# Inverting the 16-column diagonal blocks of a delta-rule stage with one block per partition, laid out through DRAM, and moving large elementwise products off GpSimd

## The chip, the cores and the metric

One core of a Trainium2 chip runs the whole kernel. The metric is device time in microseconds (us) of one execution. Engines are named as in the profile: PE is TensorE, PEld its weight loads, DVE is VectorE, ACT is ScalarE, POOL is GpSimd, SP is SyncE, whose instruction queue (SPq) issues nearly all DMAs of this kernel.

## The reference

A two-layer decoder trunk on 1024 tokens of width 1024: an MLA attention layer, an RWKV-7 layer, a feed-forward net behind each, and in both layers attention over 256 memory tokens. The change lies in the RWKV-7 layer, whose heart is a recurrence over tokens for 12 heads of width 64:

```
def step(S, inp):
    r_t, w_t, k_t, v_t, a_t, b_t = inp
    sa = jnp.einsum("bhij,bhj->bhi", S, a_t)
    S = S * w_t[:, :, None, :] + sa[..., None] * b_t[:, :, None, :] + v_t[..., None] * k_t[:, :, None, :]
    y = jnp.einsum("bhij,bhj->bhi", S, r_t)
    return S, y
```

Its result `y` is normalised per head, scaled and shifted (`rwkv_gn_g`, `rwkv_gn_b`), given a term `(r*k*r_k).sum()*v`, and gated.

## The kernel before

The recurrence is computed in chunks of `CH` = 64 tokens. A unit `n` (12 in all, `N = 2 * NPAIR`) covers two pairs of heads (`u`), four chunks (`c`, `NC` = 4) and, on the two halves of the partitions (`A`, `B`, in code `R, hd in HD`), two heads of a pair: 16 matrices of 64x64. Inside a chunk the recurrence becomes a triangular system, so every unit needs the inverse of 16 unit-triangular 64x64 matrices (identity minus the tile `N`).

The stage has these functions, in the order that the loop at its end (L1197 to L1221) calls them for each unit: `sequence(n)` carries the state through the four chunks, on PE with DVE copies between; `invert(n + 1)` makes `X`, the inverse that `sequence(n + 1)` multiplies by at L1152; `prepare(n + 2)` loads and normalises; `finish(n)` does the group norm and writes to `o_d`; `products(n + 2)` calls `unit`, which makes the scaled operands (`F`, `AR`, `BKz`) and, by the matmuls `ps_ga` (L1038), the tile `N`. Between them stand pieces of independent work, handed out by `fill` and the table `FILL`: input projections (`ps_in`), memory attention (`ps_ms`), parts of the output projection (`ps_o`), nearly all of it matmuls over 512 columns at L149 to L151.

The program is ordered by a scheduler, which places every instruction on its engine by planned durations. An engine then runs its instructions strictly in that order: one that waits holds all that stand behind it. The same holds for SPq: a DMA that waits for its source or buffer holds the DMAs behind it.

`invert` before has two parts. First it inverts the 16x16 diagonal blocks of all matrices (L1064 to L1090): POOL masks `N` to its diagonal blocks (`nx`), DVE sums them together (`ndg`), and then 15 elimination steps run in four groups. For each group ACT scales rows with columns of an identity (`Z`, L1077), a matmul with the constant `B16` spreads them over the 16 partitions of a block (`ps_z`, L1079), ACT copies the result out (`Nr`, L1081), and POOL does a product (`xtmp`, L1086) and a sum (`Xs`, L1087) for each step, 128 partitions by 120 down to 8 elements. DVE spreads the result to `X` (L1089). Then two rounds (masks `M1`, `M2`) join blocks of 16 into 32 and 64, each with a DVE transpose `XT` (L1095), matmuls `ps_q` (L1099) and `ps_x` (L1105), and DVE products.

Other products on POOL in the stage: `pm` in `shifted` (L702), the softmax weights of memory attention (L773), `F` and half of `AR` in `unit` (L1026 to L1028), and two on `o` in `finish` (L1193, L1194).

Of the kernel before, what the change touches and what calls it, by code (L numbers as in the profile page):

```python
# [10 lines left out]
F32 = mybir.dt.float32  # L11
# [9 lines left out]
P = 128  # L21
# [45 lines left out]
class Trunk:  # L67
# [588 lines left out]
    def rwkv(self, rows_src):  # L656
        nc, a, sm = self.nc, self.a, self.sm
        res_src = rows_src
        NC = QT // CH
# [5 lines left out]
        with ExitStack() as so:  # L665
# [24 lines left out]
            def shifted(ps, m, h, out, pr=None):  # L690

                pm = shp.tile([P, H], F32, name="pm", bufs=1)
                if pr is None:
                    pr = shp.tile([P, H + 1], F32, name="pr", bufs=2)
                    nc.scalar.copy(pr[:, 1:], ps)
                if h == 0:
                    nc.gpsimd.memset(pr[:, 0:1], 0.0)  # L697
                    carry[m] = sm.tile([P, 1], F32, name="carry", tag="carry", bufs=8)
                    nc.gpsimd.tensor_copy(carry[m], pr[:, H : H + 1])
                else:  # L700
                    nc.gpsimd.tensor_copy(pr[:, 0:1], carry[m])
                nc.gpsimd.tensor_scalar(pm, pr[:, 0:H], self.col("mu", m), None, op0=ALU.mult)  # L702
                nc.vector.scalar_tensor_tensor(out, pr[:, 1:], omu[:, m : m + 1], pm, op0=ALU.mult, op1=ALU.add)

            def weights(m, pool=None):
# [40 lines left out]
            def remember():  # L746
# [10 lines left out]
                def soft(n):  # L757
                    u, i = n // 4, n % 4
                    m, q, pe = u // 2, qs[u % 2], part(pes, n)
                    if i == 0:  # L760
                        nc.sync.dma_start(q, q_d[:, m, (u % 2) * H : (u % 2 + 1) * H])
                    ps = psm.tile([P, 2, NM], F32, name="ps_ms", tag="mm")
                    for hd in range(2):
                        nc.tensor.matmul(ps[:, hd, :], q[:, i * P : (i + 1) * P], mk[:, 2 * m + hd, :], start=True, stop=True)
                    nc.scalar.copy(pe, ps)
                    mx = sm.tile([P, 2], F32, name="mmx")
                    l = sm.tile([P, 2], F32, name="ml")
                    nc.vector.tensor_reduce(mx, pe, axis=AX.X, op=ALU.max)
                    nc.vector.tensor_scalar(mx, mx, -MEM_SCALE, None, op0=ALU.mult)
                    for hd in range(2):  # L770
                        nc.scalar.activation(pe[:, hd, :], pe[:, hd, :], AF.Exp, bias=mx[:, hd : hd + 1], scale=MEM_SCALE, accum_out=l[:, hd : hd + 1])
                    nc.vector.reciprocal(l, l)
                    nc.gpsimd.tensor_mul(pe, pe, l[:, :, None].broadcast_to([P, 2, NM]))  # L773

                def weigh(n):
                    u, i = n // 4, n % 4
# [129 lines left out]
            with ExitStack() as s:  # L906
# [12 lines left out]
                MM, blk, B16 = (cm[:, i, :] for i in (0, 2, 3))  # L919
# [4 lines left out]
                m16 = kp.tile([P, 80], F32, name="m16")  # L924
                nc.sync.dma_start(m16, a["consts"][:, 2690:2770])
                eye16, dg16 = m16[:, 0:16], m16[:, 16:80]
# [5 lines left out]
                self.pad(kp, 32)  # L932
                self.pad(tp, 96)
                ARK = [kp.tile([P, 2, NC, 2, P], F32, name=f"ARK{i}") for i in range(2)]
                BKz = kp.tile([P, NC, 2, P], F32, name="BKz")
                for t in [cmp_, BKz]:
                    nc.gpsimd.memset(t, 0.0)
                c3 = lambda t: t.rearrange("p (c t) -> p c t", t=CH)
                t1 = lambda name, bufs=1, tag=None: tp.tile([P, QT], F32, name=name, tag=tag or name, bufs=bufs)
                DU = {}  # L940
# [65 lines left out]
                def unit(d, u, rkv, sga, kk):  # L1006
# [16 lines left out]
                    AR = tp.tile([P, NC, 2, CH], F32, name="AR")  # L1023
                    F = tp.tile([P, NC, 2, CH], F32, name="F")
                    nc.vector.scalar_tensor_tensor(AR[:, :, 0, :], c3(kk), -1.0, pt[:, :, 0:CH], op0=ALU.mult, op1=ALU.mult)
                    nc.gpsimd.tensor_mul(F[:, :, 0, :], c3(kk), c3(at))  # L1026
                    nc.gpsimd.tensor_mul(F[:, :, 1, :], c3(k), c3(tk))
                    nc.gpsimd.tensor_mul(AR[:, :, 1, :], c3(r), pt[:, :, 1:])  # L1028

                    bz = lambda hd: bkz[:, :, hd, :].rearrange("p c (h t) -> p c h t", h=2)  # L1030
                    nc.vector.tensor_mul(bz(0)[A], F[A], c3(pi)[A][:, :, None, :].broadcast_to([64, NC, 2, CH]))
# [23 lines left out]
                    nc.vector.tensor_mul(d["bv"][:, u, :], pbv, v)  # L1055


                def invert(n):
                    d = DU[n]
                    U8 = 2 * NC  # L1060
                    N = d["N"]
                    n8 = N.rearrange("p u c t -> p (u c) t")

                    nx = up.tile([P, U8, 4, 16], F32, name="nx", bufs=1)  # L1064
                    nc.gpsimd.tensor_mul(nx.rearrange("p a b t -> p a (b t)"), n8, dg16[:, None, :].broadcast_to([P, U8, 64]))
                    ndg = up.tile([P, U8, 16], F32, name="ndg", bufs=1)
                    nc.vector.tensor_reduce(ndg, nx.rearrange("p a b t -> p a t b"), axis=AX.X, op=ALU.add)
                    Xs = up.tile([P, U8, 16], F32, name="Xs", bufs=1)
                    nc.gpsimd.tensor_copy(Xs, eye16[:, None, :].broadcast_to([P, U8, 16]))
                    for t0 in range(0, 15, 4):  # L1070

                        tn, w0 = min(4, 15 - t0), 15 - t0
                        n0 = tn * U8 * w0
                        rows = lambda t: t[:, :n0].rearrange("p (j a t) -> p j a t", j=tn, a=U8)
                        Z = up.tile([P, 480], F32, name="Z", bufs=1)
                        for j in range(tn):
                            nc.scalar.activation(rows(Z)[:, j], ndg[:, :, t0 + 1 :], AF.Copy, scale=eye16[:, t0 + j : t0 + j + 1])  # L1077
                        pz = psi.tile([P, 480], F32, name="ps_z", tag="i")
                        nc.tensor.matmul(pz[:, :n0], B16, Z[:, :n0], start=True, stop=True)  # L1079
                        Nr = up.tile([P, 480], F32, name="Nr")  # L1080
                        nc.scalar.copy(Nr[:, :n0], pz[:, :n0])  # L1081
                        for j in range(tn):
                            t = t0 + j
                            w = 15 - t
                            tmp = up.tile([P, U8, 16], F32, name="xtmp", bufs=1)
                            nc.gpsimd.tensor_mul(tmp[:, :, 0:w], rows(Nr)[:, j, :, j:], Xs[:, :, t : t + 1].broadcast_to([P, U8, w]))  # L1086
                            nc.gpsimd.tensor_add(Xs[:, :, t + 1 :], Xs[:, :, t + 1 :], tmp[:, :, 0:w])  # L1087
# [80 lines left out]
                def finish(n):  # L1168
# [14 lines left out]
                    rs2 = self.rsqrt(vr, 8, "gn")  # L1183
                    nc.vector.tensor_mul(y8, y8, rs2[:, :, None].broadcast_to([P, 8, CH]))
                    o = tp.tile([P, 2, QT], F32, name="o", tag="o")
                    for u in range(2):
                        po = psx.tile([64, NC, P], F32, name="ps_yo", tag="x")
                        for c in range(NC):
                            nc.tensor.transpose(po[:, c, :], d["yd"][:, u, c, :], self.ident)
                        for R, hd in HD:  # L1190
                            j = 2 * (pa + u) + hd
                            nc.scalar.activation(c3(o[R, u, :]), po[:, :, R], AF.Identity, scale=self.col("gng", j)[0:64, :], bias=self.col("gnb", j)[0:64, :])
# [614 lines left out]
def pack(inputs):  # L1807
# [5 lines left out]
    def put(name, m):  # L1813
        vec[:, _COLS[name] : _COLS[name] + m.shape[1]] = m
# [17 lines left out]
    for n, src in [("w0", "rwkv_w0"), ("a0", "rwkv_a0"), ("kk", "rwkv_k_k"), ("ka", "rwkv_k_a"), ("rk", "rwkv_r_k")]:  # L1832
        put(n, colz(f(src)[0].reshape(-1), 6))
    for n, src in [("gng", "rwkv_gn_g"), ("gnb", "rwkv_gn_b")]:
        v = f(src)[0].reshape(12, 64).T
        m = np.zeros((P, 12), np.float32)
        m[:64] = v
        m[64:] = v
        put(n, m)
# [72 lines left out]
```

## Time and profile before

| | us |
|---|---|
| median of 3 runs | 2696.44 (2692.29 to 2699.43) |
| the profiled execution | 2700.91 |
| its span, first to last instruction | 2699.1 |
| PE busy | 2564.5 (95% of the span) |
| DVE, ACT, POOL busy | 1803.9, 1266.7, 429.8 |
| the stretch with the recurrent stage, 1350 to 2000 us | PE 583.66, DVE 436.37, ACT 321.38, POOL 294.63 of 650 |

A view by line groups instructions that share a source line, engine and tiles; it gives their count, their busy time together, the mean of one in ns, and the idle time of the engine just before them with what ended it. A matmul on 32-bit operands leaves two records, so a count of PE records can be twice that of instructions. Busy time counts overlapping records of an engine once. A timeline gives start and duration in us in order of time. For a DMA the profile gives the time that its issue takes on SPq, and the time from issue to landing.

### The profile page before, as it was taken

How to read it: one execution, taken by the hardware profiler on the slowest of the kernel's cores; microseconds unless marked ns; L12 is line 12 of the kernel's file. 1: busy time of each engine (PE TensorE's matmuls, PEld its weight loads, DVE VectorE, ACT ScalarE, POOL GpSimd, SP SyncE). 2: the span in 40 equal slices, each digit the busy share in tenths (PEclk: the TensorE clock that was granted, in tenths of full speed). 3: DMA queues.
4: the chain of work that ended last, by engine and by line, in shares of the span. 5: the costliest groups of instructions: out<-in, count | busy, mean ns of one | idle time of the engine just before them, and what ended most of it. 6: DMA issues, size and time to landing. Idle time of an engine off the chain costs nothing.

```text
span 2699.1 us, 40995 instructions
## 1 busy us (share of the span) xinstructions
PE 2564.5 (95%) x15709; PEld 2073.5 (77%) x15709; DVE 1803.9 (67%) x3195; ACT 1266.7 (47%) x2242; POOL 429.8 (16%) x703
## 2 busy tenths in 40 slices
PE   8999999999999999999989999888998999999998
PEld 7877777778888788887877777666767888878886
DVE  5566766577565696675356566667868756568677
ACT  4465554254444433357344444665527444443343
POOL 0012232000000000002353463354310000000000
PEclk9999999999999999999999999899999999999999
DMA  4100002334443867535521222213114444386762
GB/s 168 57 28 15 9 21 84 115 106 164 152 148 137 317 240 272 189 116 210 202 92 52 63 87 67 80 52 137 53 44 160 164 152 149 137 315 242 270 226 73
DMA packets 233732, 362.13 MB, mean 134 GB/s; under 512 B 14336, under 2 KB 113024, under 8 KB 233536
## 3 DMA queue, kind: packets, MB, share of 16 engines
q1 hardware_dynamic: 233392, 359.25, 38.3%
q8 instruction: 124, 2.03, 0.3%
q14 instruction: 72, 0.59, 0.1%
q10 hardware_dynamic: 144, 0.26, 0.0%
HBM read 254.86 MB, written 104.60 MB: 133 GB/s over the span
## 4 chain that ended last, share of the span: by engine, by line
PE 81%; DVE 9%; ACT 3%; DMA 3%; issue 2%; POOL 1%; SPq 0%; DVEq 0%; ACTq 0%; POOLq 0%
PE ps_f L1290 20%; PE ps_y L1628 13%; PE ps_z L1628 10%; PE ps_in L149 4%; PE ps_in L150 4%; PE ps_in L151 4%; PE ps_o L647 2%; PE ps_pt L638 2%; PE ps_o L149 2%; PE ps_o L150 2%; PE ps_o L151 2%; PE ps_ga L1038 1%; PE ps_s L613 1%; PE ps_s L615 1%; PE ps_s L614 1%
## 5 line engine op out<-in xcount | busy, mean ns | idle before, releaser
L143 ACT CAST Xh<-wraw 128x1024 fp32r<-128x1024 f32 (+1 forms) x138 | 139.8, 1038 | 213.3 <-PE ps_z L1628 72.4
L149 PE MATMUL ps_in<-Xh,whi 128*128 128x512 f32 x480 | 195.5, 410 | 11.8 <-ACT whi L143 8.2
L150 PE MATMUL ps_in<-Xl,whi 128*128 128x512 f32 x480 | 193.6, 403 | 0.6 <-DVE Xl L144 0.6
L151 PE MATMUL ps_in<-Xh,wlo 128*128 128x512 f32 x480 | 192.9, 403 | 0.0
L143 ACT CAST Xl<-wraw 128x1024 fp32r<-128x1024 f32 x103 | 104.9, 1050 | 152.8 <-PE ps_z L1628 61.6
L144 DVE TENSOR_TENSOR Xh<-wraw,Xh 128x1024 fp32r<-128x1024 f32 x115 | 137.7, 1219 | 48.1 <-ACT Xh L143 47.7
L144 DVE TENSOR_TENSOR Xl<-wraw,Xl 128x1024 fp32r<-128x1024 f32 x103 | 123.4, 1219 | 35.7 <-ACT Xl L143 35.2
L144 DVE TENSOR_TENSOR wlo<-wraw,whi 128x1024 fp32r<-128x1024 f32 (+3 forms) x93 | 106.6, 1147 | 59.0 <-ACT whi L143 58.3
L143 ACT CAST whi<-wraw 128x1024 fp32r<-128x1024 f32 (+3 forms) x93 | 88.2, 953 | 103.6 <-PE ps_in L150 36.1
L149 PEld LDWEIGHTS ps_in<-Xh,whi 128*128 128x128 f32 x480 | 92.3, 192 | 33.5 <-ACT whi L143 8.2
L628 POOL TENSOR_TENSOR E<-E,l 128x768 f32<-128x768 f32 (+5 forms) x60 | 83.7, 1399 | 201.5 <-DVE l L626 101.3
L1290 PE MATMUL ps_f<-Xh,N 128*128 128x512 f32 x320 | 106.8, 397 | 4.9 <-ACT N L143 2.4
L697 POOL MEMSET wraw<- 128x1 f32 x2 | 0.2, 99 | 679.4 <-DMA wraw<-h_d 679.3
L150 PEld LDWEIGHTS ps_in<-Xl,whi 128*128 128x128 f32 x480 | 92.2, 192 | 19.6 <-DVE Xl L144 1.3
L151 PEld LDWEIGHTS ps_in<-Xh,wlo 128*128 128x128 f32 x480 | 92.0, 192 | 19.6 <-issue 0.6
L625 ACT ACTIVATE E<-ps_s,mx,SC 128x128 f32<-128x128 f32 (+7 forms) x96 | 79.5, 832 | 50.8 <-DVE mx L623 24.2
L1290 PE MATMUL ps_f<-TB,N 128*128 128x512 f32 x384 | 91.9, 389 | 0.3 <-ACT N L143 0.3
L1628 PE MATMUL ps_y<-Xh 128*128 128x512 f32 x384 | 90.1, 389 | 0.0
L1628 PE MATMUL ps_z<-Xh 128*128 128x512 f32 x384 | 89.6, 389 | 0.0
L1628 PE MATMUL ps_z<-Xl 128*128 128x512 f32 x384 | 89.6, 389 | 0.0
L1628 PE MATMUL ps_y<-Xh,Xh 128*128 128x512 f32 x360 | 85.0, 390 | 0.0
L1290 PEld LDWEIGHTS ps_f<-TB,N 128*128 128x128 f32 x384 | 72.0, 188 | 15.6 <-ACT N L143 0.7
(525 smaller groups left out, 6989.4 us busy)
## 6 DMA issues: line engine op xcount, KB each, us to landing
wraw<-in_w_ff_dram SPq DMA_DIRECT2D x182, 512.0 KB, 4.8
wraw<-h_d SPq DMA_DIRECT2D x108, 512.0 KB, 6.9
h_d<-slot SPq DMA_DIRECT2D x128, 256.0 KB, 2.0
h_d<-tr SPq DMA_DIRECT2D x64, 256.0 KB, 2.0
wraw<-in_w_in_dram SPq DMA_DIRECT2D x31, 512.0 KB, 4.0
lo_d<-l_st SPq DMA_DIRECT2D x36, 256.0 KB, 2.2
rkv_d<-rkv_st SPq DMA_DIRECT2D x36, 256.0 KB, 2.3
rkv<-rkv_d SPq DMA_DIRECT2D x24, 384.0 KB, 3.8
```

The lines of the kernel that those rows point to most:

```text
L143: h = self.nc.scalar.copy(hi, src)
L144: l = self.nc.vector.tensor_sub(lo, src, f32(hi))
L149: mm(ps, wh, xh, start=first, stop=False)
L150: mm(ps, wh, xl, start=False, stop=False)
L151: mm(ps, wl, xh, start=False, stop=last)
L613: nc.tensor.matmul(o, qh[:, isl], kh, start=True, stop=False)
L625: nc.scalar.activation(E3[:, g, :], S[:, g * w0 : g * w0 + n], AF.Exp, bias=mx[:, g : g + 1], scale=SC[:, i : i + 1], accum_out=l[:, g : g ...
L628: nc.gpsimd.tensor_mul(E3, E3, l[:, :, None].broadcast_to([P, nh, n]))
L638: nc.tensor.transpose(pt[:, j, :], E3[:, g, (j0 + j) * P : (j0 + j + 1) * P], self.ident)
L647: nc.tensor.matmul(po[64 * hd : 64 * hd + 64, i4 * P : (i4 + 1) * P], V[:, j, (2 * pr + hd) * 64 : (2 * pr + hd + 1) * 64], pts[hd][:, j, ...
L1290: yield nc.tensor.matmul(ps, A[x][:, k, :], B[y][:, k, :], start=fresh and k == 0 and i == 0, stop=k == 3 and i == 2, skip_group_check=True)
L1628: m = nc.tensor.matmul(ps[t], A[x][:, u, t * P : (t + 1) * P], B[y][:, u, :], start=fresh and i == u == j == 0, stop=end and i == last_ an ...
```

## The change

Four edits:

1. The first part of `invert` is replaced. The two halves of `N` are stored to a DRAM tile `nd`; eight DMAs read the diagonal 16x16 blocks back into `nb`, 64 partitions of 16x16 elements, so that each partition holds one whole block (64 blocks: 16 matrices of 4). POOL copies `nb` to `xb`, does 14 steps of a product and a sum on 64 partitions (14 to 56 elements each), and sets the diagonal to one. Eight DMAs store the blocks to a DRAM tile `xd`, which was zeroed once at the start, and two load `X` from it. `ps_z`, `Z`, `Nr`, `nx`, `ndg` and the DVE product that made `X` are gone, and so is a small constant tile. The joining rounds stay as they are.
2. `pm` goes from POOL to ACT; the softmax product, `F`, half of `AR` and the two products on `o` go from POOL to DVE.
3. In `finish`, eight PE transposes of 128x64 into 64x128 become sixteen 64x64 matmuls with an identity, which leave both heads on their own halves of the partitions; four ACT instructions on 64 partitions become two on 128. The packing of two constant columns changes with it.
4. Padding of one pool is larger.

```diff
-                nc.gpsimd.tensor_scalar(pm, pr[:, 0:H], self.col("mu", m), None, op0=ALU.mult)
+                nc.scalar.activation(pm, pr[:, 0:H], AF.Copy, scale=self.col("mu", m))
...
-                    nc.gpsimd.tensor_mul(pe, pe, l[:, :, None].broadcast_to([P, 2, NM]))
+                    nc.vector.tensor_mul(pe, pe, l[:, :, None].broadcast_to([P, 2, NM]))
...
+                PITCH = 16 * QT * 2 + 16
+                ND, XD = ([self.dp.tile([8, PITCH], F32, name=f"{c}{i}") for i in range(2)] for c in ("nd", "xd"))
...
-                    nc.gpsimd.tensor_mul(F[:, :, 0, :], c3(kk), c3(at))
-                    nc.gpsimd.tensor_mul(F[:, :, 1, :], c3(k), c3(tk))
-                    nc.gpsimd.tensor_mul(AR[:, :, 1, :], c3(r), pt[:, :, 1:])
+                    nc.vector.tensor_mul(F[:, :, 0, :], c3(kk), c3(at))
+                    nc.vector.tensor_mul(F[:, :, 1, :], c3(k), c3(tk))
+                    nc.vector.tensor_mul(AR[:, :, 1, :], c3(r), pt[:, :, 1:])
...
                 def invert(n):
-                    nc.gpsimd.tensor_mul(nx.rearrange("p a b t -> p a (b t)"), n8, dg16[:, None, :].broadcast_to([P, U8, 64]))
-                    nc.vector.tensor_reduce(ndg, nx.rearrange("p a b t -> p a t b"), axis=AX.X, op=ALU.add)
-                    for t0 in range(0, 15, 4):
...
-                        nc.tensor.matmul(pz[:, :n0], B16, Z[:, :n0], start=True, stop=True)
...
+                    for R, hd in HD:
+                        nc.sync.dma_start(rows_of(nd, hd), N[R].rearrange("p u c t -> p (u c t)"))
+                    for h in range(8):
+                        nc.sync.dma_start(nb[8 * h : 8 * h + 8], blocks_of(nd, h))
+                    nc.gpsimd.tensor_copy(xb, nb)
+                    for t in range(1, 15):
+                        w = 15 - t
+                        tmp = up.tile([64, 56], F32, name="xtmp", bufs=1)[:, : t * w].rearrange("p (s w) -> p s w", s=t)
+                        nc.gpsimd.tensor_mul(tmp, nb[:, t : t + 1, t + 1 :].broadcast_to([64, t, w]), xb[:, 0:t, t : t + 1].broadcast_to([64, t, w]))
+                        nc.gpsimd.tensor_add(xb[:, 0:t, t + 1 :], xb[:, 0:t, t + 1 :], tmp)
+                    nc.gpsimd.memset(xb.rearrange("p s t -> p (s t)")[:, 0:256:17], 1.0)
+                    for h in range(8):
+                        nc.sync.dma_start(blocks_of(xd, h), xb[8 * h : 8 * h + 8])
                     d["X"] = X = up.tile([P, 2, NC, CH], F32, name="X")
+                    for R, hd in HD:
+                        nc.sync.dma_start(X[R].rearrange("p u c t -> p (u c t)"), rows_of(xd, hd))
...
-                            nc.tensor.transpose(po[:, c, :], d["yd"][:, u, c, :], self.ident)
+                            for R, hd in HD:
+                                nc.tensor.matmul(po[R, u, c, :], d["yd"][R, u, c, :], self.ident[R, R], start=True, stop=True)
...
-                    nc.gpsimd.tensor_add(o, o, d["bv"])
-                    nc.gpsimd.tensor_mul(o, o, gt)
+                    nc.vector.tensor_add(o, o, d["bv"])
+                    nc.vector.tensor_mul(o, o, gt)
```

The scheduler lays the whole stage out anew. Three places of its order follow; in each row stand line, operation, tile written, tiles read, shape.

PE, unit 0, the end of the wait for its inverse, up to the first matmul of the joining rounds (`ps_q<-XT`). Before:

```order
L151 MATMUL ps_in<-Xh_7557,wlo 128x512
L1079 MATMUL ps_z<-Z,cm 128x72
L978 MATMUL ps_kT<-cst,cmpk 128x128
L984 MATMUL ps_kb<-kT,cm 128x128 x4
L1099 MATMUL ps_q<-XT,N 64x64 x8
L1054 MATMUL ps_bv<-rkk,cm 128x256
L1038 MATMUL ps_ga<-AR,BKz 128x128 x8
L1105 MATMUL ps_x<-X,Q 64x64 x8
```

And now:

```order
L151 MATMUL ps_in<-Xh_7557,wlo 128x512
L1093 MATMUL ps_q<-XT,N 64x64 x8
L982 MATMUL ps_kT<-cst,cmpk 128x128
L1099 MATMUL ps_x<-X,Q 64x64 x8
L988 MATMUL ps_kb<-kT,cm 128x128 x4
L1093 MATMUL ps_q<-XT,N 64x64 x8
L1058 MATMUL ps_bv<-rkk,cm 128x256
```

The `ps_z` matmuls are gone, and the first `ps_q<-XT` moved ahead of `ps_kT` and `ps_kb`, so five matmuls of `prepare` that stood before it now stand behind it.

SPq, around the inverse of unit 1. Before:

```order
L113 DMA wraw<-in_w_in_dram 128x8x128
L716 DMA rkv_d<-rkv_st 128x512
L963 DMA sga<-lo_d 128x2x256 x2
L960 DMA rkv<-rkv_d 128x3x256 x2
L716 DMA rkv_d<-rkv_st 128x512
```

And now:

```order
L967 DMA sga<-lo_d 128x2x256 x2
L1070 DMA nd_10875<-N 64x512
L964 DMA rkv<-rkv_d 128x3x256
L1070 DMA nd_10875<-N 64x512
L1072 DMA nb<-nd_10875 8x16x16 x8
L964 DMA rkv<-rkv_d 128x3x256
L716 DMA rkv_d<-rkv_st 128x512
L1081 DMA xd_10877<-xb 8x16x16 x8
L1084 DMA X<-xd_10877 64x512
L716 DMA rkv_d<-rkv_st 128x512
L1084 DMA X<-xd_10877 64x512
```

The twenty DMAs of the inverse stand among the loads and stores that were there: a load of `rkv` between the two stores of `N`, and a store of a projection (`rkv_d<-rkv_st`, which waits for DVE) between the two loads of `X`.

## Rows read from the trace of the kernel before

**Rows 1.** The page: span, PE's share, and the last chain by engine.

```profile
span 2699.1 us, 40995 instructions
PE 2564.5 (95%) x15709; PEld 2073.5 (77%) x15709; DVE 1803.9 (67%) x3195; ACT 1266.7 (47%) x2242; POOL 429.8 (16%) x703
PE 81%; DVE 9%; ACT 3%; DMA 3%; issue 2%; POOL 1%; SPq 0%; DVEq 0%; ACTq 0%; POOLq 0%
```

**Rows 2.** Stretches: length, PE, PEld, DVE, ACT, POOL busy, clock, DMA share, GB/s.

```profile
1350.00:2000.00 650.00, 583.66 (x5901) 457.51 (x5899) 436.37 (x1123) 321.38 (x824) 294.63 (x576) 0.95 0.23 74
...
1800.00:1850.00 50.00, 42.26 (x456) 33.39 (x457) 34.01 (x97) 28.61 (x83) 23.78 (x47) 0.83 0.14 43
```

**Rows 3.** By line, 1250 to 2150 us: count, busy us, mean ns, idle before.

```profile
L1079 PE MATMUL ps_z<-Z,cm 128*128 128x480 f32 (+3 forms) x96 | 35.8, 456 | 2.2 <-ACT Z L1077 2.2
...
L1189 PE MATMUL ps_yo<-cst,yd 128*64 128x128 f32 x96 | 15.4, 286 | 4.5 <-ACT o L1192 1.9 <-DVE kk L988 1.4 <-DVE yd L1184 1.1
...
L1105 PE MATMUL ps_x<-X,Q 64*64 64x64 f32 x768 | 33.7, 225 | 4.8 <-DVE Q L1101 4.7
...
L1152 PE MATMUL ps_q<-Rs,X 64*64 64x64 f32 x384 | 25.6, 238 | 2.0 <-DVE X L1106 1.5 <-DVE Rs L1140 0.6
...
L1077 ACT ACTIVATE Z<-ndg,m 128x120 f32<-128x120 f32 (+3 forms) x180 | 50.2, 349 | 3.1 <-DVE ndg L1067 3.0
...
L1101 DVE TENSOR_TENSOR Q<-ps_q,cm 128x256 f32<-128x256 f32 x48 | 20.0, 417 | 1.8 <-PE ps_q L1099 1.4
...
L1184 DVE TENSOR_TENSOR yd<-yd,rsq_y 128x512 f32<-128x512 f32 x12 | 8.3, 688 | 0.2
...
L702 POOL TENSOR_SCALAR pm<-pr,vec 128x512 f32<-128x512 f32 x39 | 72.9, 1870 | 49.5 <-ACT pr L695 43.3 <-ACT kT L980 2.5 <-DVE sh L703 1.8
```

**Rows 4.** Timelines of POOL and DVE, units 2 and 10: start, us, instruction.

```profile
1476.63 1.29 POOL L1065 TENSOR_TENSOR nx<-N,m 128x512 f32<-128x512 f32 x1 [6.73 <-ACT N L1040]
...
1508.01 0.68 DVE L1089 TENSOR_TENSOR X<-Xs,m 128x512 f32<-128x512 f32 x1
...
1896.60 1.28 POOL L1065 TENSOR_TENSOR nx<-N,m 128x512 f32<-128x512 f32 x1 [6.16 <-ACT N L1040]
...
1911.05 0.32 POOL L1087 TENSOR_TENSOR Xs<-Xs,xtmp 128x72 f32<-128x72 f32 x1
1911.45 0.31 POOL L1086 TENSOR_TENSOR xtmp<-Nr,Xs 128x64 f32<-128x64 f32 x1
...
1917.12 0.69 DVE L1089 TENSOR_TENSOR X<-Xs,m 128x512 f32<-128x512 f32 x1 [0.42 <-POOL Xs L1087]
```

**Rows 5.** One tile's instructions (`xtmp`): duration min/median/max in ns.

```profile
L1086 POOL TENSOR_TENSOR xtmp<-Nr,Xs x180: 215/322/1230, 1389.1 to 1966.1; 128x120 f32<-128x120 f32 x12, 128x112 f32<-128x112 f32 x12, 128x104 f32<-128x104 f32 x12, 128x96 f32<-128x96 f32 x12
```

**Rows 6.** DMAs: a store (L1482), loads of `sga` and of constants; issue ns, landing us.

```profile
L1482 SPq DMA_DIRECT2D h_d<-slot x128: 319/320/1519, 584.1 to 2377.8; - x128
...
DMA to landing us min/median/max: 2.0/2.0/7.0
...
L963 SPq DMA_DIRECT2D sga<-lo_d x24: 359/370/487, 1336.1 to 1883.6; - x24
...
DMA to landing us min/median/max: 2.6/2.7/7.1
...
m<-in_consts_dram SPq DMA_DIRECT2D x1, 40.0 KB, 3.9
```

**Rows 7.** SPq's waits, 1350 to 2000 us: us in total, times, longest.

```profile
SPq L963 <- POOL F L1026: 97.9, 16, 26.1
SPq L960 <- DVE bv L1055: 88.1, 8, 22.9
SPq L716 <- DVE rkv_st L703: 62.0, 14, 17.4
```

**Rows 8.** PE's waits in the same stretch, those for the inverse and for POOL.

```profile
PE ps_q L1099 <- DVE XT L1095: 4.3, 3, 2.3
...
PE ps_mpt L780 <- POOL F L1026: 1.2, 1, 1.2
```

**Rows 9.** Timeline of PE: matmuls over 512 columns, one behind the other.

```profile
1505.09 0.39 PE L151 MATMUL ps_in<-Xh,wlo 128*128 128x512 f32 x1
1505.31 0.39 PE L149 MATMUL ps_in<-Xh,whi 128*128 128x512 f32 x1
```

More of the change, by code (lines that the diff above doesn't have):

```diff
@@ L918, in rwkv @@
                 nc.sync.dma_start(cm.rearrange("p a b -> p (a b)"), a["consts"][:, 1664:2688])
-                MM, blk, B16 = (cm[:, i, :] for i in (0, 2, 3))
+                MM, blk = (cm[:, i, :] for i in (0, 2))
                 M1, M2 = cm[:, 1, 0:CH], cm[:, 1, CH:P]
@@ L923, in rwkv @@
                 nc.sync.dma_start(hsel, a["consts"][:, 2688:2690])
-                m16 = kp.tile([P, 80], F32, name="m16")
-                nc.sync.dma_start(m16, a["consts"][:, 2690:2770])
-                eye16, dg16 = m16[:, 0:16], m16[:, 16:80]
                 rm = kp.tile([P, QT], F32, name="rm")
@@ L931, in rwkv @@
                 cmp_ = kp.tile([P, P], F32, name="cmpk")
-                self.pad(kp, 32)
+                self.pad(kp, 96)
                 self.pad(tp, 96)
@@ L937, in rwkv @@
                     nc.gpsimd.memset(t, 0.0)
+                PITCH = 16 * QT * 2 + 16
+                ND, XD = ([self.dp.tile([8, PITCH], F32, name=f"{c}{i}") for i in range(2)] for c in ("nd", "xd"))
+                rows_of = lambda t, hd: t.rearrange("a b -> (a b)")[4 * PITCH * hd : 4 * PITCH * hd + 64 * 512].rearrange("(s f) -> s f", f=512)
+                blocks_of = lambda t, h: t[h, 0 : 16 * 512].rearrange("(s u t) -> u s t", s=16, u=8)[:, :, 0:16]
+                for t in XD:
+                    nc.sync.dma_start(t.rearrange("a b -> (a b)").rearrange("(p f) -> p f", p=P), BKz.rearrange("p c h t -> p (c h t)")[:, 0 : PITCH // 16])
                 c3 = lambda t: t.rearrange("p (c t) -> p c t", t=CH)
@@ L1059, in invert @@
                     d = DU[n]
-                    U8 = 2 * NC
                     N = d["N"]
-                    n8 = N.rearrange("p u c t -> p (u c) t")
-                    nx = up.tile([P, U8, 4, 16], F32, name="nx", bufs=1)
-                    nc.gpsimd.tensor_mul(nx.rearrange("p a b t -> p a (b t)"), n8, dg16[:, None, :].broadcast_to([P, U8, 64]))
-                    ndg = up.tile([P, U8, 16], F32, name="ndg", bufs=1)
-                    nc.vector.tensor_reduce(ndg, nx.rearrange("p a b t -> p a t b"), axis=AX.X, op=ALU.add)
@@ L1068, in invert @@
-                    Xs = up.tile([P, U8, 16], F32, name="Xs", bufs=1)
-                    nc.gpsimd.tensor_copy(Xs, eye16[:, None, :].broadcast_to([P, U8, 16]))
-                    for t0 in range(0, 15, 4):
[L1072 to L1078, printed above, removed]
-                        nc.tensor.matmul(pz[:, :n0], B16, Z[:, :n0], start=True, stop=True)
[L1080 to L1087, printed above, removed]
@@ new lines, in invert @@
+                    nd, xd = ND[n % 2], XD[n % 2]
+                    nb = up.tile([64, 16, 16], F32, name="nb", bufs=1)
+                    xb = up.tile([64, 16, 16], F32, name="xb", bufs=1)
+                    for R, hd in HD:
[3 more added lines that the diff above has]
+                    nc.gpsimd.tensor_copy(xb, nb)
@@ L1088, in invert @@
+                    for h in range(8):
+                        nc.sync.dma_start(blocks_of(xd, h), xb[8 * h : 8 * h + 8])
                     d["X"] = X = up.tile([P, 2, NC, CH], F32, name="X")
-                    nc.vector.tensor_mul(X.rearrange("p u c (b t) -> p (u c) b t", t=16), Xs[:, :, None, :].broadcast_to([P, U8, 4, 16]),
-                                         dg16.rearrange("p (b t) -> p b t", t=16)[:, None, :, :].broadcast_to([P, U8, 4, 16]))
+                    for R, hd in HD:
+                        nc.sync.dma_start(X[R].rearrange("p u c t -> p (u c t)"), rows_of(xd, hd))
@@ L1185, in finish @@
                     o = tp.tile([P, 2, QT], F32, name="o", tag="o")
+                    po = psx.tile([P, 2, NC, CH], F32, name="ps_yo", tag="x")
                     for u in range(2):
-                        po = psx.tile([64, NC, P], F32, name="ps_yo", tag="x")
                         for c in range(NC):
-                            nc.tensor.transpose(po[:, c, :], d["yd"][:, u, c, :], self.ident)
-                        for R, hd in HD:
-                            j = 2 * (pa + u) + hd
-                            nc.scalar.activation(c3(o[R, u, :]), po[:, :, R], AF.Identity, scale=self.col("gng", j)[0:64, :], bias=self.col("gnb", j)[0:64, :])
-                    nc.gpsimd.tensor_add(o, o, d["bv"])
-                    nc.gpsimd.tensor_mul(o, o, gt)
+                            for R, hd in HD:
+                                nc.tensor.matmul(po[R, u, c, :], d["yd"][R, u, c, :], self.ident[R, R], start=True, stop=True)
+                    for u in range(2):
+                        j = pa + u
+                        nc.scalar.activation(c3(o[:, u, :]), po[:, u], AF.Identity, scale=self.col("gng", j), bias=self.col("gnb", j))
+                    nc.vector.tensor_add(o, o, d["bv"])
+                    nc.vector.tensor_mul(o, o, gt)
                     nc.sync.dma_start(self.o_d[pa * P : (pa + 2) * P, gs].rearrange("(u i) t -> i u t", i=P), o)
@@ L1834, in pack @@
     for n, src in [("gng", "rwkv_gn_g"), ("gnb", "rwkv_gn_b")]:
[L1835 to L1839, printed above, removed]
+        put(n, colz(f(src)[0].reshape(-1), 6))
     invf = (10000.0 ** (-np.arange(16) * 2.0 / 32)).astype(np.float32)
```

## The prediction

> **What bounds the kernel now.** I read the page first. PE is busy for 95% of the span, and the chain that ended last runs on PE for 81%, DVE for 9%, POOL for 1% [rows 1]. So a change pays if it takes work from PE or a wait that PE feels; freeing POOL pays nothing by itself. Next I read the busy time of the stretch that the change touches, 1350 to 2000 us: PE works 583.66 of 650 us, so 66 us are idle there, at a mean granted clock of 0.95 [rows 2]. In one slice, 1800 to 1850 us, PE is idle for 7.7 us and the granted clock is 0.83: part of the slice ran at 1.2 GHz instead of 2.4 [rows 2]. Of the idle time, little is owed to what the change removes: the first matmuls of the joining rounds waited for `XT` 4.3 us in all, and PE waited for a product of POOL once, 1.2 us [rows 8]. The wait for the old inverse is thus mostly hidden already, behind PE work that the scheduler put there. Three questions follow: how much PE work goes, how long the new inverse takes from `N` to `X`, and how much PE work still stands in front of `X`.
>
> **PE work.** The `ps_z` matmuls go: 96 records, 35.8 us busy [rows 3]. The transposes of `finish` go too, 15.4 us [rows 3]. In their place come 12 units of 16 matmuls of 64x64, two records each, 384 in all. No such matmul against an identity stands here in the old trace, so I bound it by its neighbours: `ps_x`, of the same shape and also issued in a row on alternating halves, costs 33.7 / 768 = 0.044 us a record; `ps_q<-Rs,X`, issued in small groups, 25.6 / 384 = 0.067 [rows 3]. That is 16.9 to 25.6 us. I take 16.9, since the new order keeps most of the 16 together. Net on PE: 35.8 + 15.4 - 16.9 = 34.3 us less, at least 25.6. Stretches at half clock are in these figures as they ran.
>
> **The new inverse, N to X.** Before, I read it from the start of `nx`, which begins as `N` is complete, to the end of the DVE product that makes `X`. Unit 2: 1508.01 + 0.68 - 1476.63 = 32.1 us. Unit 10: 1917.12 + 0.69 - 1896.60 = 21.2 us [rows 4]. All 12 lie between 21 and 33 us, about 28 on average; the long ones queue behind other POOL work. After, it is a chain of four DMA trips with POOL between them:
> - Two stores of `N`: two issues at 0.32 us and a landing of 2.0 us, by the store at L1482 [rows 6]: 2.6.
> - Eight loads of `nb`: issues of 0.36 to 0.37 us one behind the other on SPq, 2.9, and the landing of the last. No transfer of 64-byte rows is in the trace; `sga` lands after 2.6 us at best, and the 40 KB of constants, the nearest in size, took 3.9 [rows 6]. So 5.5 to 6.8.
> - POOL: one copy (0.3 to 0.5 us), 28 small operations, one memset (0.1). Each operation waits for the one before; two neighbours of 72 and 64 elements start 0.40 us apart [rows 4], and the smallest durations are 0.215 us against a median of 0.322 [rows 5]. I take 0.36 from start to start, so 10.1, and 10.6 in all. Shorter rows on half the partitions could make it 8.5.
> - Eight stores of `xb`: 2.6 of issue and 2.0 of landing: 4.6.
> - Two loads of `X`: 0.7 and 2.6 to 3.9: 3.3 to 4.6.
>
> Sum: 2.6 + 5.5 + 10.6 + 4.6 + 3.3 = 26.6 us, or 29.2 with the slower landings. That is 2 us below to 1 us above the old mean, but some 5 to 8 us above the old short units such as unit 10.
>
> **The cover.** Between the last `ps_ga` of a unit (then DVE and ACT make `N` of it, about 1.5 us) and its first `ps_q<-XT` I counted the instructions on PE in both orders and gave each the distance from start to start that its kind has in the trace; matmuls over 512 columns, the bulk, start 0.22 us apart at full clock [rows 9] and 0.25 on average. It comes to 22 to 39 us, mean 30, before, and 22 to 38, mean 27, after. The excerpts of the order show one reason: without `ps_z`, and with five matmuls moved behind, unit 0 has some 4 us less in front of its inverse. The need is about 1.5 + 26.6 + 0.5 (transpose) = 28.6 us at best. PE loses a tenth to other waits anyway, which lengthens the cover to about 30. Three or four units (0, 6, 10, perhaps 8), with 22 to 25 us counted, fall short by 2 to 5 us, and four more by 1 or 2. That is 12 to 20 us of new wait in front of the joining rounds, of which 4.3 us existed. I take 18 us more.
>
> **What costs nothing.** ACT gains 24 `pm` in the stretch at about the 0.6 us of its own copies and loses `Z`, 50.2 us [rows 3], and more; it is busy half the time. DVE gains 72 products of 128x256 at 0.417 (30 us), 24 of `o` and 16 softmax products at 0.688 (28 us) [rows 3], and loses `ndg` and the old `X` product, about 21 us: 436 becomes about 473 of 650, 67% to 73%. These products run where POOL's slower ones stood (`pm` took 1.87 us there, [rows 3]), so the path through `unit` gets shorter, not longer; but DVE's copies of the state now queue a little more. I set both at nothing, 8 us either way. Should DVE's queue not hide them, the bound is the 37 us added. The 244 extra DMAs cost SPq 90 us of issue, an engine that mostly waits.
>
> **The sum.** 34 less work, 18 more wait: 16 us less, from 2700.9 us of the profiled execution to 2685. The median of the runs shown is 4.5 us below the profiled one, so I forecast 2696.4 - 16 = 2680 us.
>
> **Rivals.**
> *The cover holds.* Four trips at the quickest rows and a POOL chain of 8.5 us make the inverse 24.5 us, below the old mean, and POOL, free of other work, no longer makes it queue. Then PE saves its 34 us and some 6 us of the old waits: 2656. For it: the old trace hid a chain of 28 us nearly whole [rows 8]. Against it: the scheduler has taken 3 us of cover per unit away.
>
> *Wait for work.* New waits of 34 us, 2.9 us for each of 12 units, eat all: 2696. The landings of 3.9 us with a chain of 29.2 would do it.
>
> *SPq holds the chain (slower).* Twenty more DMAs per unit stand in a queue that runs strictly in order, with entries between them that wait for DVE or PE. In the old trace such entries held SPq for long: loads of `sga` 97.9 us in 16 waits, stores of `rkv_d` 62.0 us in 14, 4.4 us each [rows 7]. The order now has such a store between the two loads of `X` of unit 1. Before, a queue that was held only delayed prefetches; now it delays the inverse, and behind `XT` the copies of the state wait in DVE's queue, and PE with them. One wait of 4.4 us in each of 12 units is 53 us; if half the units have cover for it, 26: 2680 + 26 = 2706, and 2733 if none has. It decides from 1.3 us per unit on (16 / 12). Against it: the scheduler placed these entries by the same clock as the chain, so they should mostly be ready.
>
> *DVE stretches the chain (slower).* A POOL operation of the old inverse took 0.215 us at the least and 1.23 at the most [rows 5], so something beside it holds it up. The Trainium skill, GPSIMD Engine Reference, Specifications, says that GpSimd shares its SBUF interfaces with VectorE and contends with DVE instructions that have two SBUF inputs. The products that move to DVE have two SBUF inputs. If each of 28 operations lost 0.2 us, the chain would grow by 5.6 us a unit; over the nine units that have no cover to spare that is 50 us: 2730. The old median of 0.322 us beside a DVE that was 67% busy speaks against so much.
>
> **How the numbers follow.** About 0.3% (8 us) is what a measurement of this kernel tells from no change, so faster means below 2688. Forecast, 2666 to 2688: 0.38. Cover holds: 0.18. Wait for work, 2688 to 2704: 0.20. SPq: 0.18. DVE's contention: 0.06. Faster 0.56, same 0.20, slower 0.24. The range goes from 2645 (the quick chain, and 11 us for DVE and the shorter path through `unit`) to 2720 (SPq holding two units in three).
>
> **What would show it.** In the profile after, `ps_z` must be gone and `ps_yo` at 17 to 26 us; PE busy in the stage should fall by 26 to 34 us. From the last copy of `N` to the last landing of `X` should be 25 to 31 us; PE's and DVE's waits for `X` should total 15 to 25 us. If the waits for `X` go past 35 us, I was wrong on cover or queue: SPq's waits between `nd` and `X` then tell the queue from slow landings, and `xtmp` above 0.4 us would show DVE's contention. If the clock falls below 0.83 in many slices, the waits cost more than they last.

## The result and the profile after

The changed kernel takes 2686.6 us (median of 18 runs, 2682.3 to 2694.4), the kernel before beside it 2701.6 us (18 runs). The ratio is 0.9949 with a 95% interval of 0.9939 to 0.9959: 14 us faster, 11 to 16. The forecast was 16 us. The sum came out; the experiments below show that its terms did not. The scheduler makes a new order for every kernel here, the experiments included, so a difference between two kernels holds the effect of the new order too; the last experiments show how large that can be.

The page of the changed kernel, its span and the busy time, share and instruction count of each engine (for PE before see [rows 1]):

```profile
span 2684.7 us, 41293 instructions
PE 2543.4 (95%) x15901; PEld 2064.7 (77%) x15901; DVE 1795.9 (67%) x3283; ACT 1219.9 (45%) x2032; POOL 222.2 (8%) x525
```

POOL lost half of its work, and yet DVE, which got much of it, is busy 8 us less than the 1803.9 us before. That is the first thing which the prediction can't explain. Instruction by instruction, those that stand in both kernels took 34 us less in sum.

The stretches: busy time of PE, PEld, DVE, ACT, POOL, granted clock, DMA share, GB/s (the first answers to [rows 2]):

```profile
1350.00:2000.00 650.00, 580.90 (x6164) 463.61 (x6164) 439.86 (x1234) 265.85 (x601) 124.67 (x420) 0.93 0.30 88
1850.00:1900.00 50.00, 41.90 (x440) 32.36 (x438) 36.77 (x85) 17.67 (x36) 17.82 (x42) 0.84 0.39 115
...
1950.00:2000.00 50.00, 38.45 (x434) 31.11 (x433) 31.00 (x77) 9.21 (x12) 0.00 (x0) 0.83 0.17 54
```

PE's idle time in this stretch did not shrink (66 us before, 69 now), and the clock fell from 0.95 to 0.93.

Groups by line, 1250 to 2150 us (answering to [rows 3] and [rows 5], which have `ps_x`, `ps_q<-Rs,X` and `xtmp` of before):

```profile
L1077 POOL TENSOR_TENSOR xtmp<-nb,xb 64x14 f32<-64x14 f32 (+6 forms) x168 | 56.2, 335 | 12.9
L1078 POOL TENSOR_TENSOR xb<-xb,xtmp 64x14 f32<-64x14 f32 (+6 forms) x168 | 54.1, 322 | 12.1
...
L1099 PE MATMUL ps_x<-X,Q 64*64 64x64 f32 x768 | 34.7, 233 | 12.3 <-DVE Q L1095 12.1
L1093 PE MATMUL ps_q<-XT,N 64*64 64x64 f32 x768 | 34.5, 229 | 9.5 <-DVE rsq_t L164 5.0 <-DVE XT L1089 3.8 <-DVE rsq_t L165 0.8
...
L1146 PE MATMUL ps_q<-Rs,X 64*64 64x64 f32 x384 | 25.9, 244 | 10.3 <-DVE Rs L1134 6.3 <-DVE X L1100 4.0
...
L1089 DVE STREAM_TRANSPOSE XT<-X 128x256 f32<-128x256 f32 x48 | 21.0, 438 | 22.1 <-DMA X<-xd 22.0
...
L1184 PE MATMUL ps_yo<-cst,yd 64*64 64x64 f32 x384 | 15.2, 228 | 1.0 <-DVE yd L1178 0.8 <-DVE kk L992 0.2
```

`ps_z` is gone and `ps_yo` costs PE no more than before. DVE waits 22.0 us for `X`, but PE only 3.8 us for `XT` (and 5.8 where DVE had small operations of `rsq_t` in front of it). What grew are short waits inside the joining rounds and the sequence: for `Q` from 4.7 to 12.1 us, for `Rs` from 0.6 to 6.3.

The new chain of unit 0, whose `N` is complete at 1386.4: SPq, then the start and the end of POOL's part, then DVE (start, us, instruction, idle before):

```profile
1386.44 0.46 SPq L1070 DMA_DIRECT2D nd<-N  x1
1387.41 2.87 SPq L1072 DMA_DIRECT2D nb<-nd  x8
...
1403.79 2.86 SPq L1081 DMA_DIRECT2D xd<-xb  x8
1406.81 1.61 SPq L1084 DMA_DIRECT2D X<-xd  x2
```

```profile
1391.85 0.40 POOL L1073 COPY xb<-nb 64x256 f32<-64x256 f32 x1 [6.44 <-DMA nb<-nd]
1392.32 1.07 POOL L1077 TENSOR_TENSOR xtmp<-nb,xb 64x14 f32<-64x14 f32 x1
...
1403.54 0.22 POOL L1078 TENSOR_TENSOR xb<-xb,xtmp 64x14 f32<-64x14 f32 x1
```

```profile
1410.62 0.45 DVE L1089 STREAM_TRANSPOSE XT<-X 128x256 f32<-128x256 f32 x1 [1.33 <-DMA X<-xd]
```

From `N` to the transpose of `X` it takes 24.2 us here. Over the 12 units, from the end of the last copy of `N` to the start of `XT`, the mean is 26.8 us (23.2 to 35.9), against 29.1 before (21.3 to 33.9).

**A budget of the span.** The trace holds the times at which TensorE was granted 1.2 GHz. I split each span in three: PE's busy time as if all at 2.4 GHz (its busy time less half of what fell into those stretches), that half (the cost of the low clock), and the idle time. "Inverse only", "rest only", "idle matmuls" and "idle POOL" are experiments below.

| us | work at 2.4 GHz | low clock | idle | span |
|---|---|---|---|---|
| before | 2515.3 | 49.2 | 134.6 | 2699.1 |
| changed | 2489.3 | 54.1 | 141.3 | 2684.7 |
| inverse only | 2487.9 | 59.1 | 151.4 | 2698.4 |
| rest only | 2516.2 | 32.6 | 129.1 | 2677.9 |
| changed, idle matmuls | 2515.4 | 42.5 | 126.8 | 2684.7 |
| rest only, idle POOL | 2516.7 | 49.9 | 148.3 | 2714.9 |

### The profile page after: what moved, and what is told of

Same layout as the page of the kernel before. It is cut to its first block, busy times and chain, and to the rows that moved or that the text cites. A ratio compares the mean times of both kernels' runs of the same rounds, so it can differ in the third digit from the quotient of the medians.

```text
span 2684.7 us, 41293 instructions
## 1 busy us (share of the span) xinstructions
PE 2543.4 (95%) x15901; PEld 2064.7 (77%) x15901; DVE 1795.9 (67%) x3283; ACT 1219.9 (45%) x2032; POOL 222.2 (8%) x525
## 5 line engine op out<-in xcount | busy, mean ns | idle before, releaser
L149 PE MATMUL ps_in<-Xh,whi 128*128 128x512 f32 x480 | 195.8, 410 | 14.5 <-ACT whi L143 8.8
L150 PEld LDWEIGHTS ps_in<-Xl,whi 128*128 128x128 f32 x480 | 92.7, 193 | 19.2 <-DVE Xl L144 1.0
L1623 PEld LDWEIGHTS ps_z<-Xl 128*128 128x128 f32 x384 | 72.1, 188 | 15.0
```

Of the source, the lines that this page charges most:

```text
L149: mm(ps, wh, xh, start=first, stop=False)
L150: mm(ps, wh, xl, start=False, stop=False)
L1623: m = nc.tensor.matmul(ps[t], A[x][:, u, t * P : (t + 1) * P], B[y][:, u, :], start=fresh and i == u == j == 0, stop=end and i == last_ an ...
```

## The experiments

**Each half of the change alone.** Inverse only puts the old lines for `pm`, the softmax product, `F`, `AR`, `o` and `finish` back into the changed kernel; rest only puts the new ones into the kernel before:

```diff
-                nc.gpsimd.tensor_scalar(pm, pr[:, 0:H], self.col("mu", m), None, op0=ALU.mult)
+                nc.scalar.activation(pm, pr[:, 0:H], AF.Copy, scale=self.col("mu", m))
-                    nc.gpsimd.tensor_mul(F[:, :, 0, :], c3(kk), c3(at))
+                    nc.vector.tensor_mul(F[:, :, 0, :], c3(kk), c3(at))
...
-                    nc.gpsimd.tensor_mul(o, o, gt)
+                    nc.vector.tensor_mul(o, o, gt)
```

> The changed kernel with its large products put back on GpSimd and the old transposes in finish: only the inverse is new. Theory A (the gain is the spread matmuls ps_z that leave PE, and the new inverse is about as long as the old): 8 to 18 us below before, PE busy about 20 to 30 us below before, and the stretch from N to XT 27 to 31 us, since pm of 1.9 us queues in front of the block steps on POOL. Theory B (the gain comes from the products that left GpSimd, and the new inverse is worth nothing by itself): within 5 us of before or slower.

Measured: 2699.9 us, ratio 1.0005 (0.9990 to 1.0020). No gain at all. PE busy was 17.5 us below before, and the stretch from `N` to `XT` 32.1 us, both just outside what theory A expected.

> The kernel before with the products moved to ACT and DVE and the new finish, and with the old inverse. Theory A: within 6 us of before; ps_z stays on PE, and the old inverse gets 2 to 5 us shorter because POOL is free for it, which PE hardly feels. Theory B: 10 us or more below before. A third possibility: DVE, with 37 us more work in the stage, gets in the way of the state's copies, and it is slower by 5 to 15 us.

Measured: 2680.2 us, ratio 0.9925 (0.9910 to 0.9939), 20 us faster than before, and some 6 us faster than the whole change (0.9949, 0.9939 to 0.9959; the intervals just meet). The old inverse got 3.7 us shorter (25.4 us to `XT`). My theory A falls: the gain is not in the inverse. Page and stage of inverse only:

```profile
PE 2547.0 (94%) x15613; PEld 2065.6 (77%) x15613; DVE 1779.0 (66%) x3171; ACT 1207.3 (45%) x2014; POOL 384.7 (14%) x679
```

```profile
1350.00:2000.00 650.00, 571.83 (x5858) 455.51 (x5856) 415.71 (x1117) 264.00 (x600) 249.94 (x553) 0.93 0.29 87
```

and of rest only:

```profile
PE 2548.8 (95%) x15997; PEld 2063.6 (77%) x15997; DVE 1823.5 (68%) x3307; ACT 1279.1 (48%) x2260; POOL 257.5 (10%) x549
```

```profile
1350.00:2000.00 650.00, 591.61 (x6278) 467.23 (x6277) 472.08 (x1277) 325.23 (x829) 159.74 (x443) 0.97 0.23 76
```

By the budget, inverse only took 27.4 us of work from PE, and 16.8 us came back as idle time and 9.9 as low clock. Rest only took no work away; its 21 us came from 16.6 less low clock and 5.5 less idle time.

**A longer and a shorter chain.** The changed kernel with each product of the block steps done twice, and with 13 of the 14 steps left out:

```diff
+                        nc.gpsimd.tensor_mul(tmp, nb[:, t : t + 1, t + 1 :]..., xb[:, 0:t, t : t + 1]...)
```

```diff
-                    for t in range(1, 15):
+                    for t in range(1, 2):
```

> The changed kernel with each of the 14 products of a block inverse done twice (the same result), so that the chain from N to X grows by 14 x 0.335 = 4.7 us in each of 12 units. If the work in front of the joining rounds is just used up (as the prediction counted, 22 to 38 us against a need of about 29), PE waits 25 to 45 us more and the time is as much above the changed kernel. If there is cover to spare in most units, under 10 us above.

Measured: ratio 0.9958 (0.9941 to 0.9975), 2.5 us above the changed kernel, inside the interval, though the chain from `N` to `XT` grew to 31.7 us on average, 4.9 in each unit.

> The changed kernel with 13 of the 14 block steps left out (the blocks are not inverted), so that the chain from N to X is about 10 us shorter, and all DMAs stay. It bounds what a shorter inverse could still give. If the new inverse costs PE 12 to 20 us of waits, as predicted, 10 to 20 us below the changed kernel. If the inverse is hidden already, within 5 us of it.

Measured: ratio 0.9945 (0.9927 to 0.9964), 1 us below the changed kernel, with a chain of 17.8 us, 9.0 less in each unit. Some 59 us of chain added and some 108 taken away moved the time by 3 to 4 us in all. So the length of the inverse hardly counts. But the two runs do not hold the cover fixed: the scheduler plans the length of each chain and lays the order by it. PE's matmuls between a unit's last `ps_ga` and its first `ps_q<-XT` come to 25.9 us a unit (at 2.4 GHz) in the changed kernel, 30.4 with the longer chain and 18.2 with the shorter. The cover moved with the need. What a longer chain would cost in an order that stays as it is, no run shows.

**Work that nobody waits for on PE.** The changed kernel with the four matmuls of each unit put back, results unread:

```diff
+                    for n0 in (480, 352, 224, 72):
+                        pz = psi.tile([P, 480], F32, name="ps_z", tag="i")
+                        nc.tensor.matmul(pz[:, :n0], blk, N.rearrange("p u c t -> p (u c t)")[:, :n0], start=True, stop=True)
```

> The changed kernel with four matmuls per unit put back beside the block steps, of the shapes that ps_z had (480, 352, 224 and 72 columns), whose results nobody reads: about 30 us of PE work that needs N and that nothing waits for. Theory C (PE work of this kind filled holes between dependent steps of the recurrence; taken away, it leaves idle time and stretches at 1.2 GHz): within 6 us of the changed kernel, with less idle time and a higher granted clock in the stage. If PE work sets the time, as the prediction had it, 22 to 32 us above the changed kernel.

Measured: 2686.8 us, ratio 0.9956 (0.9941 to 0.9971), 2 us above the changed kernel by the ratios and on the same span of 2684.7 us in the profile. Their group, and two stretches (columns as above; compare the second with the same slice of the changed kernel):

```profile
L1082 PE MATMUL ps_z<-N,cm 128*128 128x480 f32 (+3 forms) x96 | 30.3, 426 | 0.6 <-ACT N L1044 0.6
```

```profile
1350.00:2000.00 650.00, 594.11 (x6257) 470.37 (x6258) 440.43 (x1233) 267.56 (x604) 120.23 (x422) 0.96 0.29 88
1850.00:1900.00 50.00, 47.33 (x504) 37.00 (x506) 38.95 (x111) 16.94 (x37) 9.15 (x32) 1.00 0.33 99
```

26 us of PE work at full clock were added and nothing was lost: idle time fell by 14.5 us and the cost of the low clock by 11.6. Of the 14.5 us, 13 lie between `N` and the first `ps_q<-XT` of the units (36.8 us of idle time in the changed kernel, 23.7 here): the matmuls ran while the next inverse was on its way. At 1850 to 1900 us PE is busy 47.33 us at 1.00 where it was busy 41.90 at 0.84. So `ps_z` had filled holes. Theory C's outcome came. The order is a new one here too, but 26 us is twice what a new order is seen to cost below.

**The queue.** The changed kernel with the twenty DMAs of the inverse on ACT's queue (`nc.sync` to `nc.scalar` at L1070, L1072, L1081, L1084):

> The changed kernel with the twenty DMAs of each inverse issued by ACT instead of SP. If SP's strict order costs the new inverse what it lost against the old one (stores of N held SP's queue for 126 us in 20 waits), 5 to 10 us below the changed kernel. Theory C, by which the inverse is hidden: within 4 us, or up to 10 us above, since ACT's own work now stands behind DMAs that wait.

Measured: ratio 0.9955 (0.9939 to 0.9971), 2 us above the changed kernel, inside the interval. The move gained nothing, and the chain to `XT` was 27.7 us against 26.8. On ACT's queue the DMAs stand among ACT's own instructions, so the run does not tell what SPq's order costs by itself. SPq did hold the chain once. SPq's waits of the changed kernel (us, times, longest), and unit 9 in its timelines, where `N` is complete at 1826.7:

```profile
SPq L1070 <- ACT R L1045: 126.4, 20, 33.5
...
SPq L1081 <- POOL xb L1078: 41.4, 8, 7.7
```

```profile
1828.88 1.70 SPq L1072 DMA_DIRECT2D nb<-nd  x4
1831.01 1.64 SPq L964 DMA_DIRECT2D rkv<-rkv_d  x2
...
1834.44 0.91 SPq L738 DMA_DIRECT2D Xl<-n_d  x2
1835.39 1.59 SPq L1072 DMA_DIRECT2D nb<-nd  x4
```

```profile
1843.01 0.39 POOL L1073 COPY xb<-nb 64x256 f32<-64x256 f32 x1 [22.02 <-DMA Xl<-n_d]
```

Half of the loads stood 5 us behind larger ones and landed another 6 us after their issue; the copy began 16.3 us after `N`, where the other units took 5 to 9. It is the unit with the longest chain, 35.9 us.

**Which move.** The kernel before with only the three products of `unit` on DVE, with only `pm` on ACT, and with only what is left (softmax and `o` products on DVE, the new `finish`):

> The kernel before with only the three products of unit (F twice, half of AR) moved from GpSimd to DVE. They stand on the path from the loads to N. Theory D (the gain comes from the shorter path through unit): 8 to 15 us below before. If the gain comes from pm, which blocked GpSimd for 1.9 us at a time in front of the inverse: within 4 us of before.

> The kernel before with only pm moved from GpSimd to ACT. Theory D: within 4 us of before, with an old inverse that is 1 to 3 us shorter. The other theory: 8 to 15 us below before.

> The kernel before with only what neither of the two single moves had: the softmax product and the two products on o on DVE, and the new finish. If the moves add up (20 us for all, 6 for unit, 7 for pm), 5 to 9 us below before. If they overlap or help each other, within 3 us of before.

Measured: 0.9977 (0.9963 to 0.9990), 6 us faster; 0.9973 (0.9961 to 0.9984), 7 us faster; 1.0002 (0.9986 to 1.0017), nothing. Neither theory of the first two was right: both moves give something, and alone they sum to 13 of the 20 us. The intervals of the four runs together are as wide as the 7 us that are left, so it isn't shown that the moves help each other.

**Work that nobody waits for on POOL.** Rest only with five products in each half unit, results unread:

```diff
+                    for i in range(5):
+                        dz = up.tile([P, QT], F32, name="dz", bufs=1)
+                        nc.gpsimd.tensor_mul(dz, r, k)
```

> The old inverse with the products moved and the new finish (the run called rest only, 2680 us), and on top five products of 128x256 on GpSimd in each half unit whose results nobody reads: 120 in all, about 95 us of POOL work that no engine waits for by its data. Theory E (large products on GpSimd cost time because DVE, beside them, runs its own products of two SBUF operands slower, and because the small block steps queue behind them): 6 to 15 us above rest only, with BKz back from 404 to about 530 ns a piece. If what cost time was the wait for the results of pm and F themselves: within 4 us of rest only.

Measured: 2712.1 us, ratio 1.0063 (1.0044 to 1.0083): 32 us above rest only by the medians, 37 by the ratios and by the two profiled spans, more than any theory gave. Its page, the group of the products, and one group of DVE products:

```profile
PE 2566.6 (95%) x15997; PEld 2075.2 (76%) x15997; DVE 1852.2 (68%) x3307; ACT 1282.8 (47%) x2260; POOL 353.5 (13%) x669
```

```profile
L1031 POOL TENSOR_TENSOR dz<-rkv 128x256 f32<-128x256 f32 x120 | 98.5, 821 | 19.8 <-DMA rkv<-rkv_d 17.9
...
L1036 DVE TENSOR_TENSOR BKz<-F,pi 64x256 f32<-64x256 f32 x48 | 23.2, 498 | 1.1
```

The same group in rest only, in the changed kernel, in the kernel before and in inverse only, which kept the large products on POOL:

```profile
L1033 DVE TENSOR_TENSOR BKz<-F,pi 64x256 f32<-64x256 f32 x48 | 19.7, 429 | 1.0
```

```profile
L1037 DVE TENSOR_TENSOR BKz<-F,pi 64x256 f32<-64x256 f32 x48 | 19.4, 422 | 1.0
```

```profile
L1033 DVE TENSOR_TENSOR BKz<-F,pi 64x256 f32<-64x256 f32 x48 | 25.6, 552 | 13.4 <-POOL F L1027 12.7
```

```profile
L1037 DVE TENSOR_TENSOR BKz<-F,pi 64x256 f32<-64x256 f32 x48 | 26.3, 567 | 14.1 <-POOL F L1031 13.4
```

DVE has 3307 instructions in both pages, and they take 28.7 us longer beside the extra 98.5 us of POOL. By the budget the 37 us of span are 19.2 of idle time and 17.3 of low clock; the part of PE's idle time whose end the profile puts down to DVE grew from 49.1 to 72.7 us. No engine waited for `dz`, and a DMA did once, for 0.4 us. That POOL's products cost time without any wait for their data is shown, though the 37 us (32 by the medians) hold a new order too. A group that reads PSUM doesn't move, in rest only and in rest only beside the extra work:

```profile
L1156 DVE COPY W<-ps_q 64x128 f32<-64x128 f32 x96 | 27.5, 287 | 28.3 <-PE ps_q L1152 27.3
```

```profile
L1159 DVE COPY W<-ps_q 64x128 f32<-64x128 f32 x96 | 27.5, 287 | 40.8 <-PE ps_q L1155 39.7
```

The Trainium skill, SBUF — State Buffer, Who interferes with whom, says that a DVE instruction with two SBUF inputs contends with a GpSimd instruction that reads SBUF. The traces agree: `BKz` reads two operands in SBUF and goes from 429 to 498 ns, `W` reads PSUM and stays at 287.

Two ways lead from there to PE: the longer DVE operations, and the small block steps that queue behind large products on POOL (the chain to `XT` grew from 25.4 to 30.9 us). Against the second speak inverse only and the longer chain: PE work of 2487.9 and 2488.0 us, chains of 32.1 and 31.7 us, yet 2699.9 and 2689.5 us. They differ in POOL's large products (and `finish`, which alone gave nothing); but 10 us between them is no more than a new order is seen to cost below, so this is a hint. Nor were the waits for data small: before, DVE stood still 12.7 us for `F`, in the row of `BKz` above, and 29.4 us for `pm`. Here is the row of that wait before, then in the run with only `pm` moved:

```profile
L703 DVE SCALAR_TENSOR_TENSOR rkv_st<-pr,omu,pm 128x512 f32<-128x512 f32 x36 | 28.7, 798 | 29.7 <-POOL pm L702 29.4 <-DMA rkv_d<-rkv_st 0.2
```

```profile
L703 DVE SCALAR_TENSOR_TENSOR rkv_st<-pr,omu,pm 128x512 f32<-128x512 f32 x36 | 28.3, 786 | 24.9 <-ACT pm L702 12.4 <-DMA rkv_d<-rkv_st 12.1
```

The wait for `pm` fell to 12.4 us, and 12.1 for a DMA came in its place; `BKz` stayed at 537 ns in that run, and yet it was 7 us faster. How the 20 us split between slower DVE operations and DVE's waits for `F` and `pm` is not settled.

**Moving filler.** Rest only with `FILL` changed, since its late slices have holes:

> Rest only with one piece of filler work moved from unit 4 to unit 6 (FILL 5, 3, 11 becomes 4, 3, 12), since PE is busy for 49.97 of 50 us at 1600 to 1650 and only for 37.48 at 1700 to 1750. If holes late in the stage can be filled: 3 to 8 us below rest only. If the hole comes from a chain and not from a lack of filler: within 3 us.

> Rest only with two pieces moved, one from unit 3 and one from unit 4 to units 6 and 7 (FILL 4, 5, 3, 11, 9 becomes 3, 4, 3, 12, 10). If filler is what the late units lack: 4 to 12 us below rest only; if the early units then lack it: within 4 us or above.

Measured: 2689.2 us (0.9973, 0.9957 to 0.9988) and 2688.8 us (0.9970, 0.9958 to 0.9981), both 9 us above rest only by the medians and 12 to 13 by the ratios. The table was not what was short; moving one piece gives up half of what rest only gains. Rest only remains the fastest kernel of the study.

These two kernels do the same work as rest only, so 9 to 13 us is what a new order alone can cost here. The 27.4 us of PE work that bought nothing, the 26 us that cost nothing, the 20 us of rest only and the 37 us of extra POOL work are above it. The 6 and 7 us of the single moves, and the 6 us between rest only and the whole change, do not, and the 14 us of the whole change barely do.

## Why the prediction was right, and where it was not

The time was right, 2680 forecast and 2686.6 measured, within the range. Its reasons were mostly wrong: PE work that was worth nothing, and moves set at nothing that were worth the gain. That these two errors cancelled is luck.

- **What bounds the kernel.** This is the step that failed. I read 95% of the span and 81% of the chain as "a change pays if it takes work from PE". In this stage it doesn't: the inverse alone took 27 us of work away and gained nothing, and putting 26 us back cost nothing. Busy 583.66 of 650 us said how full PE was, not that its work was the limit; much of that work lay where PE would otherwise wait. And "freeing POOL pays nothing by itself" looked only at PE's own waits for POOL (1.2 us), not at DVE, on which PE waits most: DVE waited 29.4 us for `pm` and 12.7 for `F`.
- **PE work.** Forecast were 34.3 us, 25.6 at least; 26.0 went by the budget at 2.4 GHz, and 21.1 of busy time as it ran, since the low clock cost 4.9 more. Counting each part of PE's busy time for the first matmul that reaches it, `ps_z` took 31.3 us with it (35.8 was its group's busy time, some of it under neighbours), and `ps_yo` did not change (13.4 before, 13.3 now). As a group it measured 15.2 us, even below my lower bound of 16.9. The sign that I gave, 26 to 34 us less PE busy in the stage, failed: 583.66 became 580.90, in a stretch that holds more of the work now.
- **N to X.** Right: 26.6 us forecast from the stores on, 28.6 with what lies around, and 26.8 from `N` to `XT`. Two legs were off, in opposite ways. From `N` to POOL's copy it took 7.1 us on average, 5.2 to 6.9 in ten of the 12 units, not 8.1: the loads of one half are issued while the second store is still landing, and I had counted the last issue of each leg twice, since the landing is timed from the start of the issue. POOL took 11.9 on average, not 10.6.
- **The cover.** Wrong. 18 us of new wait were forecast; PE's waits at `ps_q<-XT` grew from 5.6 to 9.5 us, and its idle time between `N` and there fell from 40.4 to 36.8. What failed here is to count the cover as a fixed supply: it follows the planned chain, 28.0 us of matmuls a unit before, 25.9 now and 30.4 with the longer chain, whose 4.9 us more in each of 12 units cost 2.5. PE's idle time over the whole span grew by 6.7 us, and what grew lies behind DVE, in the joining rounds and the sequence.
- **What costs nothing.** Wrong, and the largest error: the moves off POOL were set at 0, 8 us either way, and are worth 20 alone and 15 on top of the inverse (1.0005 to 0.9949). I added 58 us of products to DVE and expected 473 us in the stage; it was 440, because DVE's other instructions got shorter (`BKz` 552 to 422 ns).
- **The rivals.** *Wait for work* had the right outcome for the inverse, by the wrong way: the work was eaten by many short holes and the clock, not by waits for `X`. *SPq* did hold one unit, and the time shows no such cost. *DVE stretches the chain* had the right mechanism on the wrong side: I looked for what DVE does to POOL's chain (`xtmp` stayed at 335 ns, under the 0.4 us that would have shown it), while the trace of before already showed DVE waiting for POOL. The top of the range was mis-added: eight waits of 4.4 us on 2680 give 2715, not 2720.

## What to carry to other kernels

A busy engine is the bound only if adding idle work to it costs time: put unread instructions of the disputed size beside it and look, before work is taken away at a price. Large elementwise products on GpSimd are not free because nobody waits for them; look at the means of DVE's two-operand products with and without them, and at what DVE waits for. When a change has several parts, run each half alone: here the part with the larger diff gave nothing. Where a scheduler makes a new order for each kernel, find out first what a new order of the same work is worth, and trust no smaller difference.

## What the runs showed of the hardware

- Beside 98.5 us more of GpSimd products with operands in SBUF, DVE's 3307 instructions took 28.7 us longer and the span was 37 us longer; DVE's copies from PSUM stayed at 287 ns.
- More work on TensorE went with a higher granted clock: with the same inverse, 26 us of added matmuls left 14.5 us less idle time and 11.6 us less cost of the low clock. The mean granted clock of the stage was 0.96 against 0.93.
- Eight loads of 64-byte rows, 8 KB each, had landed 1.6 us after the end of the last issue in unit 0, where POOL's copy began; that is some 1.9 us from its start, sooner than the loads of `sga` in the trace of before (2.6 us at the least from the issue on, [rows 6]).
